# Weight tiles of half the size, and the squares of the residual behind all turning, in a two-layer trunk

## The chip, the cores and the metric

One core of one Trainium2 chip runs the whole program, eight cores being there. The metric is the device time of one execution in microseconds, of which the median of several runs is given. The profile's span is counted from the first to the last instruction and is a little shorter than the execution it was taken of. Engines are named as in the profile: PE multiplies matrices (PEld loads its weights), ACT is the scalar engine, DVE the vector engine, POOL and SP here issue DMA.

## The reference

The input is x of 256 tokens by 2048. Layer 0 mixes tokens by a gated linear recurrence (HGRN2, 16 heads), layer 1 by gated linear attention (GLA, 4 heads), each in chunks of 64 tokens. Behind each mixer comes an MLP of width 8192 with a squared ReLU. Around each of the four sub-layers stand two norms and a residual:

```
for i in range(DEPTH):
    hn = rmsnorm(h, norm_mix_pre[i])
    m = hgrn2_mixer(hn, ...) if i % N_MIXERS == 0 else gla_mixer(hn, ...)   # ends in o @ w_out
    h = h + rmsnorm(m, norm_mix_post[i])
    f = sqrelu_mlp(rmsnorm(h, norm_mlp_pre[i]), mlp_w_up[i], mlp_w_down[i])
    h = h + rmsnorm(f, norm_mlp_post[i])

def sqrelu_mlp(h, w_up, w_down):
    u = jax.nn.relu(h @ w_up)
    return (u * u) @ w_down
```

All is float32, and all matrix products are wide: 2048 by 8192 (HGRN2's inputs), 2048 by 2048, 2048 by 6160 (GLA's inputs), and for each layer 2048 by 8192 and 8192 by 2048.

## The kernel before

**Splits.** PE multiplies a rounded float32 format. To keep float32's precision each operand is split into two: `hi`, a rounded copy, made by ACT (`split_hi`, line 113), and `lo`, the rest raw - hi, made by DVE (`split_lo`, line 117). A product is three matmuls, x_hi by w_hi, x_hi by w_lo and x_lo by w_hi (lines 145 to 147 in `mm_half`, line 171 and 174 in `gemmT` for products that come out turned). So every weight passes DMA, ACT and DVE before PE takes it.

**Chunks and halves.** The host lays the weights out in chunks of 1 MB, 128 partitions by 2048 numbers. `load_chunk` (line 107) takes a tile from the pool `wraw` and loads a whole chunk by one DMA from SP's queue; the pool has three such tiles. Everything behind it works in halves of 128 x 1024: a hi and a lo tile of this size come from the pool `wsp` (five of each). A raw tile can be loaded anew when the lo of its second half is made. Six kinds of loads use `wraw`, 364 whole chunks in all; SP's queue issues 435 DMAs.

**The MLP.** The rows of 256 tokens meet `w_up` in groups of eight chunks (`up`, `gemmT`). The product with `w_dn` is done block by block in a Strassen-like form, with seven products in place of eight (`seven`, line 659): some operands are sums of two weight blocks, made by DVE (line 696, 714) or by accumulating DMAs that POOL issues (line 638 `add_to`, line 650 `load_b12`) into tiles called `bs`. `step` and `plan` weave the two; the products are called sa, sb and sc.

**The passage** (`transition`, line 436) leads from the last quarter of columns of one sub-layer to the first product of the next. It is run three times: from HGRN2's output projection to MLP 0, from MLP 0 to GLA, and from GLA's output projection to MLP 1. The order on PE, ACT, DVE and POOL is written out by hand there (`manual_schedule(engines=ALL)`; SP isn't among them). For each half `t` of the tokens (128 rows): the last products (`last`), the norm (`first_use`, `post.rstd`), the four residual additions on DVE (`post.residual(n, t)`, line 386), the turning of the new residual in four blocks (`T_in(t, q)`: four transposes on PE into one of two PSUM banks, line 207; `T_out(t, q)`: split out of the bank by four instructions on ACT, line 218, and four on DVE, line 220), and then the products `nxt(t, j)`, j = 0 to 7, of the turned blocks with eight weight halves. These eight halves are split ahead (`Next`, `ahead.split()`): they go to rooms that lie idle then (sbig, sqk, sf, stt, saccA, srun in the profile), some to `wsp`. For the scale of the next norm the squares of the residual are summed on ACT (`square`, line 309, four per token half); `rstd_sum` needs all eight. `split_early` splits the first three halves of the sub-layer's own weights.

**Who sets the order elsewhere.** In `start` (line 235) a hand-written order includes SP. Everywhere else a scheduler orders the instructions of each engine by a simulated timeline, in which loads count too; so other tiles can move other instructions. Each engine's queue runs in its order.

Of the kernel before, what the change touches and what calls it, by code (L numbers as in the profile page):

```python
# [11 lines left out]
F32 = mybir.dt.float32  # L12
# [6 lines left out]
P = 128  # L19
# [11 lines left out]
def trunk(  # L31
# [7 lines left out]

    const = ctx.enter_context(tc.tile_pool(name="const", bufs=1))  # L40
    big = ctx.enter_context(tc.tile_pool(name="big", bufs=4))
    wraw = ctx.enter_context(tc.tile_pool(name="wraw", bufs=3))
    wsp = ctx.enter_context(tc.tile_pool(name="wsp", bufs=5))
    tokp = ctx.enter_context(tc.tile_pool(name="tok", bufs=12))
    halfp = ctx.enter_context(tc.tile_pool(name="half", bufs=6))
# [28 lines left out]
    def nm(s):  # L74
        uid[0] += 1
        return f"{s}_{uid[0]}"
# [26 lines left out]
    def load_chunk(wap, idx):  # L103
        if idx in ahead and ahead[idx][0] is wap:
            return ahead.pop(idx)[1]
        raw = wraw.tile([P, 2, 1024], F32, tag="raw", name=nm("raw"))
        nc.sync.dma_start(raw, wap[idx].rearrange("p (k n) -> p k n", k=2))
        return raw

    def split_hi(raw, into=None):  # L110
# [16 lines left out]
    def split_early(wap, idx, count):  # L127

        raw = load_chunk(wap, idx)
        early[wap.tensor.name, idx] = raw, [split(raw[:, hf, :]) for hf in range(count)]  # L130

    def split_chunk(wap, idx):

        raw, halves = early.pop((wap.tensor.name, idx), (None, []))
        if raw is None:
            raw = load_chunk(wap, idx)
        return halves + [split(raw[:, hf, :]) for hf in range(len(halves), 2)]

    def mm_half(ps, half, hf, xs, t, nk, kks=(0, 1), cs=slice(0, NB)):

# [94 lines left out]
    def start(which, w, base):  # L235

        X = Xhl(KT)
        xs = big.tile([P, KT, T], F32, tag="big", name="xs")  # L240
        ps = [psmm.tile([P, NB], F32, tag="mm", name=nm("mm")) for _ in range(NT)]
        first = []
        part = small.tile([P, NT, 4], F32, tag="tp", name=nm("tp"))
        new_residue()

        def input_quarters(t, qs):
            for q in qs:
                c = slice(q * NB, (q + 1) * NB)
                nc.sync.dma_start(hs(t, c), x[t * P:(t + 1) * P, c])
            for q in qs:  # L250
                square(part, t, q)

        def next_chunk(c):
            raw = wraw.tile([P, 2, 1024], F32, tag="raw", name=nm("raw"))
            for j in range(2):
                nc.sync.dma_start(raw[:, j, :], w[c].rearrange("p (k n) -> p k n", k=2)[:, j, :])
            ahead[c] = w, raw
            first.append(gemmT(w, c, X, *((psmm, "mm") if c < 2 else (pssc, "sc"))))

        with tc.manual_schedule(engines=ALL | {mybir.EngineType.SP}):  # L260
            for hf in range(KT // 2):
                if hf % 2 == 0:
                    raw = wraw.tile([P, 2, 1024], F32, tag="raw", name=nm("raw"))
                    src = w[base + hf // 2].rearrange("p (k n) -> p k n", k=2)
                for n in range(2 if hf == 0 else 1):

                    m = 2 if hf else 1
                    ks = slice(2 * hf + n, 2 * hf + n + m)
                    cs = slice(n * NB, (n + m) * NB)
                    lead = hf == 0 and n == 0  # L270
                    nc.sync.dma_start(xs[:, ks, :], xT[:, ks, :])
                    (nc.scalar if lead else nc.sync).dma_start(raw[:, hf % 2, cs], src[:, hf % 2, cs])
                    if lead:
                        nc.sync.dma_start(prew, npre)
                        A.activation(warm, epsb, AF.Sqrt)
                        for _ in range(4):
                            idle = pstr.tile([P, T], F32, tag="tr", name=nm("idle"))
                            PE.matmul(idle, bc(epsb, [P, P]), bc(epsb, [P, T]), start=True, stop=True)
                    for k in range(2 * hf + n, 2 * hf + n + m):
                        hi, lo = X.both(k)[:, 0, :], X.both(k)[:, 1, :]  # L280
                        g = prew[:, which, k:k + 1]
                        A.activation(hi, xs[:, k, :], AF.Copy, scale=g)
                        V.scalar_tensor_tensor(lo, xs[:, k, :], g, hi.bitcast(F32),
                                               ALU.mult, ALU.subtract)
                    if n == 0:
                        half = (wsp.tile([P, 1024], F32R, tag="hi", name=nm("hi")),
                                wsp.tile([P, 1024], F32R, tag="lo", name=nm("lo")))
                    A.activation(half[0][:, cs], raw[:, hf % 2, cs], AF.Copy)  # L288
                    V.tensor_tensor(half[1][:, cs], raw[:, hf % 2, cs],  # L289
                                    half[0][:, cs].bitcast(F32), ALU.subtract)  # L290
                    if hf == 0:
                        for t in range(NT):
                            mm_half(ps[t], half, hf, X, t, KT, (n,))
                if hf:
                    for t in range(NT):
                        mm_half(ps[t], half, hf, X, t, KT)
            next_chunk(0)
            next_chunk(1)
            input_quarters(0, (0, 1))
            next_chunk(2)  # L300
            input_quarters(0, (2, 3))
            nc.sync.dma_start(ident, ident_in)
            next_chunk(3)
            input_quarters(1, range(4))
            rs = rstd_sum(part)
        return X, rs, ps, first
# [81 lines left out]
    class Next:  # L388
# [27 lines left out]
                yield None  # L416

        def raw(self, j):
            return self.raws[j // 2][:, j % 2, :]

        def hi(self):
            j = len(self.parts)
            if j % 2 == 0:
                self.raws.append(load_chunk(self.w, self.base + j // 2))
            self.parts.append(split_hi(self.raw(j), next(self.room)))

        def lo(self):
# [8 lines left out]
    def transition(w, base, nk, xs, post, add, which, ahead):  # L436
# [20 lines left out]
        def nxt(t, j):  # L457
            mm_half(psn[t], ahead.parts[j], j, X, t, KT)
# [21 lines left out]
        with tc.manual_schedule(engines=ALL):  # L480
# [28 lines left out]
            nxt(0, 3)  # L509
            post.residual(1, 1)  # L510
            post.residual(2, 1)
            part = small.tile([P, NT, 4], F32, tag="tp", name=nm("tp"))
            for q in range(4):
                square(part, 0, q)
            nxt(0, 4)
            ahead.split()
            T_in(1, 0)
            T_out(1, 0)
            nxt(0, 5)
            T_in(1, 1)  # L520
            nxt(0, 6)
            T_out(1, 1)
            post.residual(3, 1)
            T_in(1, 2)
            nxt(0, 7)
            T_out(1, 2)
            T_in(1, 3)
            T_out(1, 3)
            for chunk in ahead.then:
                split_early(*chunk)  # L530
            for q in range(4):
# [7 lines left out]
    def mlp(layer, w_up, w_dn, X, rs, ps0, then=None, at_end=None):  # L539
# [119 lines left out]
        def seven(g, p, following):  # L659
# [9 lines left out]
                return lambda k: (sa[g][k][:, 0, c, :], sa[g][k][:, 1, c, :])  # L669

            def raw_of(h, n):
                raw = load_chunk(w_dn, n * 16 + 2 * g + h)
                return [raw[:, j, :] for j in range(2)]

            def product(b, x, raw, n, t, sign=1):
                banks, key = (through, p) if b == "c" else (bank, b)
# [587 lines left out]
```

## Time and profile before

| what | value |
|---|---|
| time, median of 3 runs | 2246.48 us (2246.0 to 2246.5) |
| the profiled execution | 2245.75 us, of which span 2244.0 us |
| granted clock of PE | 0.999 |
| DMA | 516.67 MB, mean 230 GB/s |
| queue q1 (SP's and ACT's loads) | 405.43 MB |
| queue q0 (POOL's) | 109.06 MB |

The page gives each engine's busy time. A busy PE alone says little here, since matmuls overlap: the waits of PE and of its weight loads, and the distance between the starts of matmuls, tell where it stood still. A wait is put down to the line and engine that ended it; a line that is a helper's, like 113 or 117, stands for all splits. In the timeline equal instructions that follow each other on an engine are one row, and what stands in brackets is the idle time ahead of it and what ended it.

### The profile page before, as it was taken

To read this page: it belongs to the slowest core of one execution; us is meant where nothing else is said; L and a number is where in the kernel's file an instruction comes from. 1 tells how busy PE (TensorE), PEld (TensorE's weight loads), DVE (VectorE), ACT (ScalarE), POOL (GpSimd) and SP (SyncE) were. 2 spreads that over 40 slices of the span, in tenths; PEclk is the share of its full clock that TensorE was granted. 3 is DMA by queue.
4 is the path that set the end of the run, shared out by engine and by line. 5 is a ranking of instruction groups with operands and counts; after the bars stand their busy time and mean duration, and the time that the engine had idled before them with its cause. 6 is when DMAs were issued, how large, how long until landed. Compare 5 with 4: busy or idle time off the path is not lost.

```text
span 2244.0 us, 30106 instructions
## 1 busy us (share of the span) xinstructions
PE 2229.9 (99%) x11380; PEld 1898.8 (85%) x11380; DVE 1823.2 (81%) x2503; ACT 1404.5 (63%) x1926; POOL 119.4 (5%) x162
## 2 busy tenths in 40 slices
PE   9999999999999999999999999999999999999998
PEld 7888888888888888888887888888888888888887
DVE  6887877667899899898886778666789989989886
ACT  7554555456666666676657456555766666667664
POOL 0000000000010110110000000000001010011000
PEclk9999999999999999999999999999999999999999
DMA  8545445457889889888863544465788988898885
GB/s 327 177 166 172 169 152 186 169 207 239 263 268 264 265 266 272 268 255 280 268 263 133 201 156 160 170 203 201 232 263 274 262 265 267 271 271 256 273 266 189
DMA packets 85233, 516.67 MB, mean 230 GB/s; under 512 B 10144, under 2 KB 10656, under 8 KB 32352
## 3 DMA queue, kind: packets, MB, share of 16 engines
q1 hardware_dynamic: 62192, 405.43, 49.7%
q0 software_dynamic: 22752, 109.06, 22.2%
q8 instruction: 89, 1.46, 0.3%
q14 instruction: 56, 0.46, 0.1%
q10 hardware_dynamic: 144, 0.26, 0.0%
HBM read 508.43 MB, written 6.29 MB: 229 GB/s over the span
## 4 chain that ended last, share of the span: by engine, by line
PE 92%; DVE 3%; DMA 3%; ACT 1%; issue 1%; SPq 0%; DVEq 0%; ACTq 0%
PE mmT L171 26%; PE mmT L174 13%; PE sa L687 12%; PE mm L146 9%; PE mm L147 9%; PE mm L145 9%; PE sb L687 6%; PE sc L687 3%; DMA raw<-w_up 2%; PE sc L858 2%; DVE lo L117 2%; ACT hi L113 1%; PE tr L207 1%; DMA raw<-w_dn 0%; PE sd L894 0%
## 5 line engine op out<-in xcount | busy, mean ns | idle before, releaser
L113 ACT ACTIVATE hi<-raw 128x1024 fp32r<-128x1024 f32 x718 | 751.4, 1058 | 534.5 <-PE mm L147 173.2
L117 DVE TENSOR_TENSOR lo<-raw,hi 128x1024 fp32r<-128x1024 f32 x718 | 865.1, 1220 | 259.9 <-ACT hi L113 192.2
L171 PE MATMUL mmT<-xhl,hi 128*128 128x512 f32 x2688 | 652.5, 391 | 0.8 <-ACT hi L113 0.7
L171 PEld LDWEIGHTS mmT<-xhl,hi 128*128 128x128 f32 x2688 | 499.4, 188 | 103.7 <-ACT hi L113 3.0
L174 PEld LDWEIGHTS mmT<-xhl,lo 128*128 128x128 f32 x2688 | 352.0, 191 | 16.1
L174 PE MATMUL mmT<-xhl,lo 128*128 128x256 f32 x2688 | 359.2, 283 | 0.0
L146 PE MATMUL mm<-lo,xhl 128*128 128x512 f32 (+1 forms) x896 | 349.5, 390 | 0.7 <-DVE lo L117 0.4
L145 PE MATMUL mm<-hi,xhl 128*128 128x512 f32 (+1 forms) x896 | 349.0, 391 | 1.2 <-ACT hi L288 0.6
L147 PE MATMUL mm<-hi,xhl 128*128 128x512 f32 (+1 forms) x896 | 347.7, 389 | 0.0
L113 ACT ACTIVATE hi<-bs 128x1024 fp32r<-128x1024 f32 x224 | 234.9, 1057 | 92.4 <-PE mmT L171 46.7
L117 DVE TENSOR_TENSOR lo<-bs,hi 128x1024 fp32r<-128x1024 f32 x224 | 270.4, 1219 | 13.7 <-PE mmT L174 8.8
L145 PEld LDWEIGHTS mm<-hi,xhl 128*128 128x128 f32 x896 | 168.9, 188 | 35.9 <-ACT hi L288 1.3
L146 PEld LDWEIGHTS mm<-lo,xhl 128*128 128x128 f32 x896 | 169.0, 189 | 35.4 <-DVE lo L289 1.4
L147 PEld LDWEIGHTS mm<-hi,xhl 128*128 128x128 f32 x896 | 168.7, 188 | 34.4 <-issue 0.3
L687 PE MATMUL sb<-hi,as 128*128 128x512 f32 x448 | 149.2, 390 | 0.0
L687 PE MATMUL sa<-hi,as 128*128 128x512 f32 x448 | 148.0, 391 | 0.0
L687 PE MATMUL sa<-hi,xhl 128*128 128x512 f32 x448 | 147.4, 390 | 0.0
L638 POOL DMA_DIRECT2D bs<-w_dn x100 | 87.3, 874 | 1012.0 <-DVE lo L117 561.6
L687 PEld LDWEIGHTS sa<-hi,xhl 128*128 128x128 f32 x448 | 84.2, 188 | 17.0
L687 PEld LDWEIGHTS sa<-hi,as 128*128 128x128 f32 x448 | 84.3, 188 | 16.3
L687 PEld LDWEIGHTS sb<-hi,as 128*128 128x128 f32 x448 | 84.3, 188 | 15.9
L687 PE MATMUL sb<-lo,as 128*128 128x512 f32 x224 | 87.9, 392 | 1.2 <-DVE lo L117 1.2
(236 smaller groups left out, 2180.1 us busy)
## 6 DMA issues: line engine op xcount, KB each, us to landing
raw<-w_up SPq DMA_DIRECT2D x128, 1024.0 KB, 5.7
raw<-w_dn SPq DMA_DIRECT2D x100, 1024.0 KB, 6.7
raw<-w_hin SPq DMA_DIRECT2D x56, 1024.0 KB, 4.9
bs<-w_dn POOLq DMA_DIRECT2D x112, 512.0 KB, 7.2
raw<-w_gin SPq DMA_DIRECT2D x48, 1024.0 KB, 4.9
bs<-w_dn POOLq DMA_DIRECT2D x44, 1024.0 KB, 8.4
raw<-w_hout SPq DMA_DIRECT2D x16, 1024.0 KB, 4.9
raw<-w_gout SPq DMA_DIRECT2D x16, 1024.0 KB, 4.9
```

The source lines that it names most:

```text
L113: A.activation(hi, raw, AF.Copy)
L117: V.tensor_tensor(half[1], raw, half[0].bitcast(F32), ALU.subtract)
L145: PE.matmul(ps, xh, hi[:, kk, cs], start=(k == 0), stop=False)
L146: PE.matmul(ps, xh, lo[:, kk, cs], start=False, stop=False)
L147: PE.matmul(ps, xl, hi[:, kk, cs], start=False, stop=(k == nk - 1))
L171: PE.matmul(ps, hi, X.both(k), start=(k == 0), stop=False)
L174: PE.matmul(ps[:, 0, :], lo, X.both(k)[:, 0, :], start=False, stop=(k == KT - 1))
L207: PE.transpose(ps[:, j, :], src(j), ident)
L638: nc.gpsimd.dma_start(raw, b, accum_op=ALU.add)
L687: PE.matmul(ps, l, r[:, kk, :], start=first and j + kk + i == 0, stop=j + kk + i == 4, skip_group_check=not first)
L858: PE.matmul(ps[:, hd, :], l(hd * kt + k), r(hd * kt + k), start=(k == 0), stop=(k == kt - 1))
```

## The change

It has two parts. The pool `wraw` gets six tiles of half a chunk in place of three of a whole one, and each half is loaded by a DMA of its own, of 512 KB; `load_chunk` returns a list of two tiles. `Next.hi` now loads only the half that it splits. In the passage, for the second token half, the four squares of the first token half go from ahead of that half's turning to behind it, the split `ahead.split()` goes from ahead of `T_in(1, 0)` to behind `T_out(1, 0)`, and the writing order of `nxt` and `T_out` becomes regular.

```diff
-    wraw = ctx.enter_context(tc.tile_pool(name="wraw", bufs=3))
+    wraw = ctx.enter_context(tc.tile_pool(name="wraw", bufs=6))
...
-        raw = wraw.tile([P, 2, 1024], F32, tag="raw", name=nm("raw"))
-        nc.sync.dma_start(raw, wap[idx].rearrange("p (k n) -> p k n", k=2))
+        return [load_half(wap[idx].rearrange("p (k n) -> p k n", k=2)[:, j, :]) for j in range(2)]
+
+    def load_half(src):
+        raw = wraw.tile([P, 1024], F32, tag="raw", name=nm("raw"))
+        nc.sync.dma_start(raw, src)
         return raw
...
-        return halves + [split(raw[:, hf, :]) for hf in range(len(halves), 2)]
+        return halves + [split(raw[hf]) for hf in range(len(halves), 2)]
...
         def hi(self):
             j = len(self.parts)
-            if j % 2 == 0:
-                self.raws.append(load_chunk(self.w, self.base + j // 2))
+            chunk = self.w[self.base + j // 2].rearrange("p (k n) -> p k n", k=2)
+            self.raws.append(load_half(chunk[:, j % 2, :]))
             self.parts.append(split_hi(self.raw(j), next(self.room)))
...
             post.residual(2, 1)
+            nxt(0, 4)
+            T_in(1, 0)
+            T_out(1, 0)
+            ahead.split()
+            nxt(0, 5)
+            T_in(1, 1)
+            T_out(1, 1)
+            post.residual(3, 1)
+            nxt(0, 6)
+            T_in(1, 2)
+            T_out(1, 2)
+            nxt(0, 7)
+            T_in(1, 3)
+            T_out(1, 3)
             part = small.tile([P, NT, 4], F32, tag="tp", name=nm("tp"))
             for q in range(4):
                 square(part, 0, q)
-            nxt(0, 4)
-            ahead.split()
-            T_in(1, 0)
-            T_out(1, 0)
-            nxt(0, 5)
-            T_in(1, 1)
-            nxt(0, 6)
-            T_out(1, 1)
-            post.residual(3, 1)
-            T_in(1, 2)
-            nxt(0, 7)
-            T_out(1, 2)
-            T_in(1, 3)
-            T_out(1, 3)
             for chunk in ahead.then:
                 split_early(*chunk)
```

`start`, `next_chunk` and `raw_of` are written to match: the first loads were cut into halves by DMA before, but into a tile of a whole chunk.

Three places in the built programs. The lines of the changed kernel are three higher (110 is its load, 116 and 120 are hi and lo) or one lower (308, 385) than those of before. The first is ACT's queue in the first passage, from the output projection to MLP 0. Before:

```order
357 L309 ACTIVATE tok_4437,tp_4436<-h_119 128x512
358 L309 ACTIVATE tok_4439,tp_4436<-h_119 128x512
359 L309 ACTIVATE tok_4441,tp_4436<-h_119 128x512
360 L309 ACTIVATE tok_4443,tp_4436<-h_119 128x512
361 L113 ACTIVATE hi_4451<-raw_4327 128x1024
362 L218 ACTIVATE xhl_4267<-tr_4455,prew 128x128 x4
363 L218 ACTIVATE xhl_4267<-tr_4474,prew 128x128 x4
364 L218 ACTIVATE xhl_4268<-tr_4494,prew 128x128 x4
365 L218 ACTIVATE xhl_4268<-tr_4513,prew 128x128 x4
366 L113 ACTIVATE hi_4528<-raw_4526 128x1024
```

And the same place of the change:

```order
358 L221 ACTIVATE xhl_4423<-tr_4600,prew 128x128 x4
359 L116 ACTIVATE hi_4615<-raw_4613 128x1024
360 L221 ACTIVATE xhl_4423<-tr_4625,prew 128x128 x4
361 L221 ACTIVATE xhl_4424<-tr_4645,prew 128x128 x4
362 L221 ACTIVATE xhl_4424<-tr_4664,prew 128x128 x4
363 L308 ACTIVATE tok_4678,tp_4677<-h_119 128x512
364 L308 ACTIVATE tok_4680,tp_4677<-h_119 128x512
365 L308 ACTIVATE tok_4682,tp_4677<-h_119 128x512
366 L308 ACTIVATE tok_4684,tp_4677<-h_119 128x512
367 L116 ACTIVATE hi_4690<-raw_4686 128x1024
```

The four squares (tok<-h) went from ahead of the four turned blocks (xhl<-tr) to behind them, and the split hi from ahead of block 0 to behind it. The same place on DVE, from the two residuals of the second token half on. Before:

```order
561 L386 SCALAR_TENSOR_TENSOR h_119<-tok_4175,col_4398,h_119 128x512
562 L117 TENSOR_TENSOR lo_4452<-raw_4327,hi_4451 128x1024
563 L220 SCALAR_TENSOR_TENSOR xhl_4267<-tr_4455,prew,xhl_4267 128x128 x4
564 L220 SCALAR_TENSOR_TENSOR xhl_4267<-tr_4474,prew,xhl_4267 128x128 x4
565 L386 SCALAR_TENSOR_TENSOR h_119<-tok_4383,col_4398,h_119 128x512
```

With the change:

```order
562 L385 SCALAR_TENSOR_TENSOR h_119<-tok_4323,col_4556,h_119 128x512
563 L223 SCALAR_TENSOR_TENSOR xhl_4423<-tr_4600,prew,xhl_4423 128x128 x4
564 L120 TENSOR_TENSOR lo_4616<-raw_4613,hi_4615 128x1024
565 L223 SCALAR_TENSOR_TENSOR xhl_4423<-tr_4625,prew,xhl_4423 128x128 x4
566 L385 SCALAR_TENSOR_TENSOR h_119<-tok_4541,col_4556,h_119 128x512
```

The split lo went behind block 0; the residual of the last quarter (row 565, now 566) still has the same work ahead of it. The third place is SP's queue within MLP 0, where loads of `w_up` and `w_dn` take turns. Before, one row is a chunk:

```order
156 L107 DMA raw_6895<-w_dn 128x2048
157 L107 DMA raw_6925<-w_up 128x2048
158 L107 DMA raw_7018<-w_up 128x2048
159 L107 DMA raw_7067<-w_dn 128x2048
160 L107 DMA raw_7098<-w_up 128x2048
```

With the change, two rows are one:

```order
278 L110 DMA raw_7139<-w_dn 128x1024
279 L110 DMA raw_7141<-w_dn 128x1024
280 L110 DMA raw_7171<-w_up 128x1024
281 L110 DMA raw_7173<-w_up 128x1024
282 L110 DMA raw_7266<-w_up 128x1024
283 L110 DMA raw_7268<-w_up 128x1024
284 L110 DMA raw_7317<-w_dn 128x1024
285 L110 DMA raw_7319<-w_dn 128x1024
286 L110 DMA raw_7350<-w_up 128x1024
287 L110 DMA raw_7352<-w_up 128x1024
```

The sequence of chunks is the same, and each half has its own row and so its own tile to wait for. The scheduler also changed the places of some splits and small PE groups in the MLPs and ahead of the passages; the amount of work on PE, ACT, DVE and POOL is the same.

More of the change, by code (lines that the diff above doesn't have):

```diff
@@ L129, in split_early @@
         raw = load_chunk(wap, idx)
-        early[wap.tensor.name, idx] = raw, [split(raw[:, hf, :]) for hf in range(count)]
+        early[wap.tensor.name, idx] = raw, [split(raw[hf]) for hf in range(count)]
     def split_chunk(wap, idx):
@@ L253, in next_chunk @@
         def next_chunk(c):
[L254 to L257, printed above, removed]
+            ahead[c] = w, load_chunk(w, c)
             first.append(gemmT(w, c, X, *((psmm, "mm") if c < 2 else (pssc, "sc"))))
@@ L261, in start @@
             for hf in range(KT // 2):
-                if hf % 2 == 0:
-                    raw = wraw.tile([P, 2, 1024], F32, tag="raw", name=nm("raw"))
-                    src = w[base + hf // 2].rearrange("p (k n) -> p k n", k=2)
+                raw = wraw.tile([P, 1024], F32, tag="raw", name=nm("raw"))
+                src = w[base + hf // 2].rearrange("p (k n) -> p k n", k=2)
                 for n in range(2 if hf == 0 else 1):
@@ L271, in start @@
                     nc.sync.dma_start(xs[:, ks, :], xT[:, ks, :])
-                    (nc.scalar if lead else nc.sync).dma_start(raw[:, hf % 2, cs], src[:, hf % 2, cs])
+                    (nc.scalar if lead else nc.sync).dma_start(raw[:, cs], src[:, hf % 2, cs])
                     if lead:
@@ L287, in start @@
                                 wsp.tile([P, 1024], F32R, tag="lo", name=nm("lo")))
-                    A.activation(half[0][:, cs], raw[:, hf % 2, cs], AF.Copy)
-                    V.tensor_tensor(half[1][:, cs], raw[:, hf % 2, cs],
+                    A.activation(half[0][:, cs], raw[:, cs], AF.Copy)
+                    V.tensor_tensor(half[1][:, cs], raw[:, cs],
                                     half[0][:, cs].bitcast(F32), ALU.subtract)
@@ L418, in raw @@
         def raw(self, j):
-            return self.raws[j // 2][:, j % 2, :]
+            return self.raws[j]
         def hi(self):
             j = len(self.parts)
-            if j % 2 == 0:
-                self.raws.append(load_chunk(self.w, self.base + j // 2))
+            chunk = self.w[self.base + j // 2].rearrange("p (k n) -> p k n", k=2)
+            self.raws.append(load_half(chunk[:, j % 2, :]))
             self.parts.append(split_hi(self.raw(j), next(self.room)))
@@ L671, in raw_of @@
             def raw_of(h, n):
-                raw = load_chunk(w_dn, n * 16 + 2 * g + h)
-                return [raw[:, j, :] for j in range(2)]
+                return load_chunk(w_dn, n * 16 + 2 * g + h)
             def product(b, x, raw, n, t, sign=1):
```

## The prediction

> **What bounds the kernel now.** The page comes first, then the windows of 50 us, then who waited for whom, and last the timeline at the waits.
>
> ```profile
> span 2244.0 us, 30106 instructions
> PE 2229.9 (99%) x11380; PEld 1898.8 (85%) x11380; DVE 1823.2 (81%) x2503; ACT 1404.5 (63%) x1926; POOL 119.4 (5%) x162
> ```
> ```profile
> 0.00:50.00 50.00, 48.14 (x214) 39.21 (x215) 32.03 (x56) 40.05 (x64) 0.20 (x4) 1.00 0.90 334
> 750.00:800.00 50.00, 49.81 (x258) 42.44 (x257) 44.09 (x54) 33.11 (x41) 6.41 (x8) 1.00 0.87 261
> 1500.00:1550.00 50.00, 50.00 (x222) 41.42 (x221) 33.26 (x35) 29.12 (x37) 0.00 (x0) 1.00 0.80 279
> 2200.00:2250.00 50.00, 36.29 (x183) 30.85 (x181) 28.30 (x42) 16.70 (x30) 0.00 (x0) 0.93 0.37 138
> ```
>
> A window's columns are its bounds, its length, the busy time (and instructions) of PE, PEld, DVE, ACT and POOL, the granted clock, the busy share of the 16 DMA engines and GB/s. PE is idle for 2244.0 - 2229.9 = 14.1 us. The first window holds 50 - 48.14 = 1.9 us of it, the last, which has 44 us of the run, 44.0 - 36.3 = 7.7 us: start and tail, which the change leaves alone. Between them lie 4.5 us. So no edit to loads or to other engines can win much; the clock is full. Busy PE hides a little more, since the ends of matmuls are modelled, so the pitch counts:
>
> ```profile
> 30.48 3.63 PE mmT L171 x16
> ```
>
> In this row of the chain of waits 16 matmuls of 512 columns take 3.63 us, 0.227 us each, though each shows some 0.39 us in the timeline. Where the next one starts later than 0.227 us after the last, PE stalled, idle or not. Who waited, first on PE, then on its weight loads, then on ACT (columns: total us, times, longest):
>
> ```profile
> PE tr L207 <- DVE xhl L220: 1.5, 4, 1.0
> PE sb L687 <- DVE lo L117: 1.2, 2, 0.6
> PE mmT L171 <- ACT hi L113: 0.7, 2, 0.5
> PE mm L146 <- DVE lo L117: 0.4, 1, 0.4
> ```
> ```profile
> PEld mmT L171 <- ACT hi L113: 3.0, 7, 0.9
> PEld sb L687 <- DVE lo L117: 2.5, 4, 1.0
> PEld mm L146 <- DVE lo L117: 0.9, 1, 0.9
> ```
> ```profile
> ACT hi L113 <- DMA raw<-w_up: 73.5, 13, 7.2
> ```
>
> PE waits for a split (hi on ACT, lo on DVE), the split for a load of `w_up`. One such place in the timeline, and its load in the chain:
>
> ```profile
> 757.39 1.22 DVE L117 TENSOR_TENSOR lo<-raw,hi 128x1024 fp32r<-128x1024 f32 x1
> ...
> 759.46 1.22 DVE L117 TENSOR_TENSOR lo<-raw,hi 128x1024 fp32r<-128x1024 f32 x1
> ...
> 760.71 3.80 SPq L107 DMA_DIRECT2D raw<-w_up  x2
> ...
> 762.93 3.49 DVE L117 TENSOR_TENSOR lo<-raw,hi 128x1024 fp32r<-128x1024 f32 x3
> ...
> 771.14 2.01 ACT L113 ACTIVATE hi<-raw 128x1024 fp32r<-128x1024 f32 x2 [6.94 <-DMA raw<-w_up]
> ...
> 771.68 0.39 PE L687 MATMUL sc<-hi,xhl 128*128 128x512 f32 x1
> ...
> 772.26 3.92 PE L171 MATMUL mmT<-xhl,hi 128*128 128x512 f32 x16 [0.19 <-ACT hi L113]
> ```
> ```profile
> 760.71 10.33 DMA raw<-w_up
> ```
>
> The load is issued at 760.71, right behind the lo that ends at 759.46 + 1.22 = 760.68: that was the second half of the chunk whose buffer it takes. It needs 10.33 us, ACT sits for 6.94 us, and PE, which had splits in hand, stalls by 772.26 - 771.68 - 0.227 = 0.35 us, between its idle 0.19 and the longer wait of its weight load.
>
> **The change, part by part.** *Halves.* The same bytes come in tiles of half a chunk, six in place of three. The first half's buffer is then free at 757.39 + 1.22 = 758.61, not at 760.68: its load is issued 2.07 us sooner, carries half the bytes, and ACT can start on it alone. The second half is issued when the chunk was. The longest of these PE waits is 1.0 us, so 2.07 us covers each. The three kinds of PE wait above add up to 1.2 + 0.7 + 0.4 = 2.3 us by PE's idle time, and to 3.0 + 2.5 + 0.9 = 6.4 us by its weight loads, which wait beside a running matmul. The pitch at 772.26 lies between the two, so I take the middle, **4.3 us saved**, and keep 0 and 6.4 as the ends. The waits of sb belong to it: there DVE is catching up after such a hold of ACT.
>
> Each chunk has one more load to issue and to wait for.
>
> ```profile
> 29.88 3.49 DVE L117 TENSOR_TENSOR lo<-raw,hi 128x1024 fp32r<-128x1024 f32 x3
> ```
> ```profile
> 774.63 0.33 SPq L107 DMA_DIRECT2D raw<-w_up  x1
> ```
> ```profile
> raw<-w_up SPq DMA_DIRECT2D x128, 1024.0 KB, 5.7
> raw<-w_hin SPq DMA_DIRECT2D x15, 512.0 KB, 7.6
> ```
>
> At 29.88 the chunks were already loaded half by half (line 256), and three lo take 3.49 us, as at 762.93 where they came whole: a wait for each half costs DVE nothing once the half is there. Behind a waiting hi stand only later splits and folds on ACT, whose half would have been waited for in any case. SP gets one more issue for each of 364 whole-chunk loads, 0.33 us each, 120 us over the whole span, on a queue with 435 issues (144 us) that otherwise waits for buffers: 0 us. If SP had no room, a load would be 0.33 us later, well inside the 2.07.
>
> Of the DMA itself: the opening window loads halves and moves 334 GB/s at a busy share of 0.90, 371 per full share; the window at 1500 loads whole chunks at 279 / 0.80 = 349. Halves cost the engines nothing that these rows show, and the busiest stage has 0.87. I take 0; the bad end is the fourth case below. [...]
>
> *The passage.* The squares issue no DMA; the split now issues its own half's load (before, the chunk had come whole with the split ahead of it), on SP, whose order isn't written by hand there and which has its buffer earlier than the split its place. In each of the three passages, four squares leave ACT's queue ahead of the second half's turning, and the split (hi and lo) slides from ahead of the first turned block of that half to behind it. The squares' own cost there is the stretch from 1177.90 to 1180.35, 2.45 us of ACT. Passage from MLP to GLA:
>
> ```profile
> 1177.90 0.67 ACT L309 ACTIVATE tok<-h 128x512 f32<-128x512 f32 x1
> ...
> 1178.99 0.60 PE L207 MATMUL tr<-ident,h 128*128 128x128 f32 x4
> ...
> 1180.35 1.08 ACT L113 ACTIVATE hi<-raw 128x1024 fp32r<-128x1024 f32 x1
> ...
> 1181.30 2.20 ACT L218 ACTIVATE xhl<-tr,prew 128x128 fp32r<-128x128 f32 x8
> ...
> 1182.61 2.15 DVE L220 SCALAR_TENSOR_TENSOR xhl<-tr,prew,xhl 128x128 fp32r<-128x128 f32 x8
> ...
> 1183.79 0.66 PE L207 MATMUL tr<-ident,h 128*128 128x128 f32 x4 [1.00 <-DVE xhl L220]
> ...
> 1184.68 0.74 DVE L386 SCALAR_TENSOR_TENSOR h<-tok,col,h 128x512 f32<-128x512 f32 x1
> ...
> 1185.67 0.60 PE L207 MATMUL tr<-ident,h 128*128 128x128 f32 x4
> ```
>
> Block 0 is turned by 1178.99 + 0.60 = 1179.59, but ACT takes it at 1181.30, behind squares and split; DVE is through with it after half of its 2.15 us, near 1183.7, and block 2, which needs that bank, waits 1.00 us. After the change ACT takes block 0 at 1179.6 and is done at 1180.8 (1.14 us a block, the row at 504.75 below), DVE 1.08 us later, 1181.9, ahead of the time at which PE wants the bank (1183.79 - 1.00 = 1182.8): that wait goes. What is late next: DVE then does lo (1.22), block 1 (1.08) and the last residual (0.74) in a row, 1181.9 + 3.0 = 1184.9, some 1185.0 with the hand-over, and block 3 can't be turned before. It was turned at 1185.67, so this passage wins **0.6 us**, not 1.0.
>
> In the two passages behind an output projection ACT had time for the squares:
>
> ```profile
> 504.75 1.14 ACT L218 ACTIVATE xhl<-tr,prew 128x128 fp32r<-128x128 f32 x4
> ...
> 508.79 0.74 DVE L386 SCALAR_TENSOR_TENSOR h<-tok,col,h 128x512 f32<-128x512 f32 x1
> ...
> 509.59 0.65 PE L207 MATMUL tr<-ident,h 128*128 128x128 f32 x4
> ...
> 511.30 2.97 ACT L113 ACTIVATE hi<-raw 128x1024 fp32r<-128x1024 f32 x3
> ```
> ```profile
> 520.99 1.29 PE L171 MATMUL mmT<-xhl,hi 128*128 128x512 f32 x5
> ```
>
> ACT takes block 0 at 504.75, straight after it is turned; nothing is to be won. Now hi (1.08) comes behind it, 505.9 to 507.0; DVE has block 0 to 507.0, lo to 508.2, block 1 to 509.3, and the residual runs to 510.0, not 509.53. Block 3 was turned at 509.59, right behind it, and so comes **0.5 us** later, twice. The squares now follow the last turning, ahead of the early splits, which start at 511.30 + 0.5 + 2.45 = 514.3 and end at 517.2; PE first needs them at 520.99, so 3.8 us of cover are left and they cost nothing. Without that cover it would be 2.45 us a passage.
>
> **Sum.** -4.3 (loads) - 0.6 + 2 x 0.5 (passages) = -3.9 us. The profiled execution took 2245.75 us, so 2241.9 for it; its median of three lies 0.7 us higher, 2246.48, hence **2242.6 us**.
>
> **The rivals.** *More goes* (0.17): with halves every one of those waits vanishes at the weight loads too, 6.4 us, and -6.4 + 0.4 gives 2240.5. For it: 2.07 us is more than each wait. Against: the wait of a weight load is partly beside a running matmul.
> *The loads are no earlier* (0.20): the 10.33 us come from engines that are 0.87 busy with the accumulating loads too, not from a late issue; then only the passages count, +0.4: 2246.9. Against: a load that is half as long and issued sooner must end sooner unless something else is pushed ahead of it.
> *Half loads land later* (0.08, the slower side): the 512 KB rows landed in 7.6 us, `w_up`'s chunks in 5.7, so 1.9 us longer. The second half is issued when the chunk was; if it is late by that much where ACT has no lead, PE's stall grows by as much. Seven places (the count at mmT) x 1.9 = 13.3 us: 2260. It decides as soon as a half lands later than its chunk did. Against: those 512 KB loads landed in the opening crowd at 0.90. [...]
>
> **Chances.** My forecast gets 0.55, from 2241.0 to 2244.5. A measurement of this kernel tells 0.2%, 4.5 us, from no change, so faster means under 2242.0. Of the forecast 0.12 lies there, with the 0.17 of the first rival 0.29. Within: 0.43 + 0.20 = 0.63. Slower: 0.08. The range 2240.0 to 2247.5 leaves out the slow case, half of the first rival and a little beyond the second.
>
> **What would show it.** In the profile after: ACT's waits for `w_up` well under 73.5 us and none near 7; PE's waits for hi and lo from loads gone (if they stand, the second rival; if longer, the third); in the MLP to GLA passage no 1.00 us before a turning by DVE's block, but a short one for the residual at block 3 in all three. Wrong would also be a stall at a place where there was none: other instructions were reordered with the loads, and I have counted that as nothing.

## The result, and the profile after

| | before | after |
|---|---|---|
| median of 6 runs, in turn on one chip | 2246.89 us (2246.0 to 2248.82) | 2258.32 us (2257.22 to 2260.48) |
| ratio, 95% interval | | 1.0051 (1.0040 to 1.0061) |
| span of the profiled execution | 2244.0 us | 2256.2 us |

The change makes the kernel 11.4 us slower; 2242.6 was predicted. The page's first lines of the changed kernel show as little as they did before:

```profile
span 2256.2 us, 31260 instructions
PE 2233.2 (99%) x11380; PEld 1901.1 (84%) x11380; DVE 1823.7 (81%) x2503; ACT 1408.7 (62%) x1926; POOL 119.8 (5%) x162
```

PE is now idle for 2256.2 - 2233.2 = 23.0 us instead of 14.1, and 3.3 us longer busy with the same 11380 matmuls. Who waited on PE, and for whom (total us, times, longest):

```profile
PE mmT L174 <- DVE tok L590: 7.3, 2, 4.3
PE mm L148 <- ACT hi L116: 1.8, 1, 1.8
...
PE sb L685 <- DVE lo L120: 1.4, 2, 0.9
...
PE tr L210 <- DVE h L385: 0.6, 3, 0.2
```

Two waits of the first row are new: `unfold` (line 590, tok<-mmT) frees a PSUM bank and comes late. The waits that were forecast to go are gone, but for sb's (1.4 us in 2, 1.2 before). DVE's own waits name a transfer that kept nobody waiting there before; two of the four are shown below, in MLP 0, the other two (4.15 and 2.99 us) stand at the same place in MLP 1:

```profile
DVE bs L694 <- DMA raw<-w_dn: 17.1, 4, 6.0
```

The n-th matmul writes the same tile in both kernels, but for 142 of the 11380, which the scheduler moved, so the difference of its starts tells where the time went (worked out from the two traces; times are those of before):

| stretch | us lost |
|---|---|
| opening, to 20 | +1.8 |
| 20 to 533 | -0.5 |
| **start of MLP 0, 533 to 554** | **+6.6** |
| 554 to 942 | -1.3 |
| 942 to 1130 (its end holds the 1.8 us wait of the second row) | +2.1 |
| 1130 to 1197, with the passage into GLA | -1.5 |
| 1197 to 1584 | +0.4 |
| **start of MLP 1, 1584 to 1616** | **+4.7** |
| 1616 to the last matmul | +0.1 |

The opening runs in an order written by hand that all kernels below with half tiles share; their profiles show -0.2 to 1.84 us there, so it isn't counted as an effect of the change. What is left, in the main, are the starts of the two MLPs. The timeline of DVE at the start of MLP 0 after the change (start, length, operation; in brackets the idle time ahead and what ended it):

```profile
536.11 1.23 DVE L694 TENSOR_TENSOR bs<-raw,bs 128x1024 f32<-128x1024 f32 x1 [5.95 <-DMA raw<-w_dn]
537.25 1.22 DVE L120 TENSOR_TENSOR lo<-raw,hi 128x1024 fp32r<-128x1024 f32 x1
...
545.32 1.23 DVE L694 TENSOR_TENSOR bs<-raw,bs 128x1024 f32<-128x1024 f32 x1 [3.98 <-DMA raw<-w_dn]
546.46 2.36 DVE L120 TENSOR_TENSOR lo<-raw,hi 128x1024 fp32r<-128x1024 f32 x2
...
550.47 0.42 DVE L590 TENSOR_TENSOR tok<-mmT,half 128x256 f32<-128x256 f32 x1
```

And of the kernel before at the same place:

```profile
539.11 2.35 DVE L696 TENSOR_TENSOR bs<-raw,bs 128x1024 f32<-128x1024 f32 x2
...
543.11 0.42 DVE L591 TENSOR_TENSOR tok<-mmT,half 128x256 f32<-128x256 f32 x1
```

Before, both additions run without a wait and the first unfold starts at 543.11; after, each addition waits for its half of `w_dn`, and the first unfold starts at 550.47, 7.4 us later (1.4 of them were lost before this place). SP's queue tells why there are two waits and not one:

```profile
530.19 8.64 SPq L110 DMA_DIRECT2D raw<-w_dn  x2
```

A row of two issues ends with the second: half 0 was asked for at 530.19, half 1 only at 530.19 + 8.64 - 0.33 = 538.50, right behind the lo of 537.25, which ends at 538.47. That lo frees half 1's tile (in the program half 1 goes to the place in SBUF that this lo reads), and it stands behind the addition that waits for half 0. PE, which needs a bank for its next product, meanwhile:

```profile
550.94 5.30 PE L174 MATMUL mmT<-xhl,hi 128*128 128x512 f32 x15 [4.32 <-DVE tok L590]
```
```profile
1622.37 5.52 PE L174 MATMUL mmT<-xhl,hi 128*128 128x512 f32 x16 [2.97 <-DVE tok L590]
```

PE idles 4.32 and 2.97 us, and then 16 matmuls take 5.52 us (the view of the first row ends ahead of its sixteenth). In the kernel before, the same row of the timeline shows 3.82:

```profile
1617.25 3.82 PE L171 MATMUL mmT<-xhl,hi 128*128 128x512 f32 x16
```

The clock had fallen. Windows of the changed kernel (columns as in the prediction):

```profile
548.00:552.00 4.00, 1.06 (x3) 0.88 (x4) 4.00 (x9) 1.64 (x4) 0.00 (x0) 0.89 0.87 141
552.00:556.00 4.00, 4.00 (x14) 3.18 (x13) 3.34 (x14) 4.00 (x12) 0.00 (x0) 0.69 0.66 252
1616.00:1620.00 4.00, 3.40 (x25) 3.04 (x23) 3.25 (x3) 2.27 (x4) 0.88 (x1) 1.00 0.68 228
1623.00:1627.00 4.00, 4.00 (x12) 3.19 (x11) 3.27 (x13) 4.00 (x11) 0.00 (x0) 0.59 0.79 286
```

In MLP 1, 2.97 us of idle time and 5.52 - 3.82 = 1.7 us of slow clock are the 4.7 us of the table. In both MLPs the next product starts 5.37 us after the first of these matmuls (556.31 and 1627.74), where it was 3.66 us before, so MLP 0 loses 1.7 us by the clock too, and idle time and clock together make 4.32 + 2.97 + 2 x 1.7 = 10.7 of the 11.4 us. The queue of DVE at the start of MLP 0, in numbered rows of the two programs; before:

```
587 L117 TENSOR_TENSOR lo_4879<-raw_4872,hi_4878 128x1024
588 L696 TENSOR_TENSOR bs_4973<-raw_4971,bs_4691 128x1024
589 L696 TENSOR_TENSOR bs_4973<-raw_4971,bs_4692 128x1024
590 L215 TENSOR_TENSOR xhl_4609<-tr_4640,xhl_4609 128x4x128
591 L117 TENSOR_TENSOR lo_4925<-raw_4922,hi_4924 128x1024
592 L591 TENSOR_TENSOR tok_4650<-mmT_4651,half_4684 128x256
```

With the change:

```
585 L694 TENSOR_TENSOR bs_5147<-raw_5143,bs_4855 128x1024
586 L120 TENSOR_TENSOR lo_4989<-raw_4982,hi_4988 128x1024
587 L218 TENSOR_TENSOR xhl_4773<-tr_4792,xhl_4773 128x4x128
588 L120 TENSOR_TENSOR lo_5045<-raw_5040,hi_5044 128x1024
589 L120 TENSOR_TENSOR lo_5049<-raw_5042,hi_5048 128x1024
590 L694 TENSOR_TENSOR bs_5147<-raw_5145,bs_4856 128x1024
591 L120 TENSOR_TENSOR lo_5097<-raw_5092,hi_5096 128x1024
592 L120 TENSOR_TENSOR lo_5101<-raw_5094,hi_5100 128x1024
593 L218 TENSOR_TENSOR xhl_4773<-tr_4804,xhl_4773 128x4x128
594 L120 TENSOR_TENSOR lo_5154<-bs_5147,hi_5153 128x1024
595 L590 TENSOR_TENSOR tok_4814<-mmT_4815,half_4848 128x256
```

The scheduler now has a separate ready time for each half. It put the first addition ahead of a lo (row 586) that used to be ahead of both, and two splits, one more of the next chunk (row 592) and that of the sum (row 594, from bs), ahead of the unfolds; before, three of the four unfolds stood ahead of both. In the timeline above DVE takes these rows in the order of its queue, from row 585 at 536.11 us to row 595 at 550.47, so everything below a row that waited came later too. ACT's queue has the same thing at the end of MLP 0 (the wait of 1.8 us):

```profile
1128.49 1.06 ACT L116 ACTIVATE sbig<-raw 128x1024 fp32r<-128x1024 f32 x1 [4.94 <-DMA raw<-w_gin]
1129.46 1.04 ACT L116 ACTIVATE hi<-bs 128x1024 fp32r<-128x1024 f32 x1
1130.40 1.04 ACT L116 ACTIVATE hi<-raw 128x1024 fp32r<-128x1024 f32 x1
```

The split of the next stage's first half (sbig) waits for `w_gin`; behind it stand the hi's that PE needs at once.

### The profile page after: what moved, and what is told of

Read it like the earlier page. It is cut to its first block, busy times and chain, and to the rows that moved or that the text cites. A ratio compares the mean times of both kernels' runs of the same rounds, so it can differ in the third digit from the quotient of the medians.

```text
span 2256.2 us, 31260 instructions
## 1 busy us (share of the span) xinstructions
PE 2233.2 (99%) x11380; PEld 1901.1 (84%) x11380; DVE 1823.7 (81%) x2503; ACT 1408.7 (62%) x1926; POOL 119.8 (5%) x162
## 4 chain that ended last, share of the span: by engine, by line
PE 93%; DVE 3%; DMA 2%; ACT 1%; issue 1%; SPq 0%; DVEq 0%; ACTq 0%
PE mmT L174 26%; PE mmT L177 13%; PE sa L685 12%; PE mm L148 9%; PE mm L149 9%; PE mm L150 9%; PE sb L685 6%; PE sc L685 3%; PE sc L856 2%; DMA raw<-w_up 2%; DVE lo L120 1%; ACT hi L116 1%; PE tr L210 1%; DVE xhl L223 1%; PE sd L892 0%
```

## The experiments

Theory T: the scheduler places the first users of a half too early into queues that run in order, and what stands behind them is late. Rivals: P, the passage's later squares delay the MLP; D, half loads themselves cost the DMA queue. Three more came up on the way: N, the loss comes wherever the queues are ordered anew; C, the first addition's wait holds up the load that the second one waits for; Q, what counts is how late the unfolds come. Each run was measured in turn with the kernel before on one chip, and the ratio is to it; the chips differ between runs. The diffs are shortened: conditions that the text names, and the unwrapping of an instruction for `issue_after`, are left out.

| run | median us | ratio (95%) |
|---|---|---|
| half tiles, old passage | 2251.02 | 1.0019 (1.0011 to 1.0028) |
| new passage, whole chunks | 2245.97 | 0.9999 (0.9990 to 1.0008) |
| all pairs joined | 2257.58 | 1.0052 (1.0039 to 1.0065) |
| all pairs joined, old passage | 2258.76 | 1.0049 (1.0036 to 1.0061) |
| first pair joined | 2246.51 | 1.0000 (0.9991 to 1.0009) |
| first pair joined, old passage | 2245.66 | 0.9999 (0.9990 to 1.0007) |
| both pins | 2243.66 | 0.9988 (0.9979 to 0.9997) |
| both pins, old passage | 2243.13 | 0.9987 (0.9978 to 0.9996) |
| addition behind the split | 2253.71 | 1.0027 (1.0016 to 1.0038) |
| half loads, whole tiles | 2244.59 | 0.9988 (0.9979 to 0.9997) |
| splits behind the unfolds | 2248.35 | 1.0003 (0.9994 to 1.0011) |
| both moves | 2246.60 | 0.9996 (0.9987 to 1.0005) |

**Each part alone.** Half tiles with the passage's order of before, that is the change without its edit to `transition`:

```diff
+            part = small.tile([P, NT, 4], F32, tag="tp", name=nm("tp"))
+            for q in range(4):
+                square(part, 0, q)
             nxt(0, 4)
+            ahead.split()
             T_in(1, 0)
             T_out(1, 0)
-            ahead.split()
...
```

> Half tiles as in the changed kernel, the passage's squares where they stood before. Theory T (in each MLP the two additions that open the first pair of blocks stand apart in VectorE's queue, each waits for its half of w_dn, and the unfolds behind them free PSUM banks late): the waits of VectorE at about 536 and 545 us stay, and the time is 2256 to 2259, as of the whole change. Rival P (the later squares delay the start of the MLP): the waits go and the time is 2243 to 2248. Rival D (half loads cost the DMA queue itself): 2256 to 2259 too, and this run alone cannot tell D from T.

```profile
PE mmT L174 <- DVE tok L590: 4.0, 2, 3.0
```

2251.0 us: half tiles alone lose, but less than half of what the change loses, so no number was met, neither that of T and D nor P's. The two waits for the bank are there, shorter (3.0 and 1.05 us against 4.32 and 2.97). The passage alone, that is the change without this:

```diff
-    wraw = ctx.enter_context(tc.tile_pool(name="wraw", bufs=6))
+    wraw = ctx.enter_context(tc.tile_pool(name="wraw", bufs=3))
...
-        return [load_half(wap[idx].rearrange("p (k n) -> p k n", k=2)[:, j, :]) for j in range(2)]
+        raw = wraw.tile([P, 2, 1024], F32, tag="raw", name=nm("raw"))
+        nc.sync.dma_start(raw, wap[idx].rearrange("p (k n) -> p k n", k=2))
...
```

> Whole chunks as before, the passage in its new order. T and D: within 1 us of the kernel before (2246 to 2248), with the bank wait of 1.0 to 1.2 us in the passage into the GLA gone and short waits for the last residual in its place. P: about 2256 to 2258.

```profile
PE tr L207 <- DVE h L386: 0.5, 3, 0.2
```

2246.0 us, no difference, as T and D said: the passage by itself costs nothing, so P as a cause by itself falls. Its own two effects came as forecast: the bank wait went, and three short waits for the last residual took its place. In its profile the matmuls run 1.6 us ahead of the kernel before at 1616 us and 0.7 behind it at the end, with one new wait of 1.2 us for a hi at 1839 us; so the new passage, too, let the scheduler change other places, and the zero is a sum.

**Joining the additions.** In `seven`, line 693 on:

```diff
-            for j in range(2):
-                V.tensor_tensor(run[j], b11[j], q[j], ALU.add)
+            second = V.tensor_tensor(run[1], b11[1], q[1], ALU.add)
+            with tc.issue_after(second):
+                V.tensor_tensor(run[0], b11[0], q[0], ALU.add)
```

> The changed kernel with one difference: the addition of the second half is placed first and that of the first half right behind it, so that unfolds stand ahead of both in VectorE's queue. T: the idle stretches of TensorE before the first matmuls at the start of both MLPs (4.3 and 3.0 us, and the slow matmuls behind them) go, the time falls by 8 to 11 us, to 2247 to 2250. D: unchanged, 2257 to 2259, with the idle time in other places. P: unchanged.

> Half tiles, the two additions joined as in the run before, and the squares of the passage where they stood before the change. T: 8 to 11 us under the changed kernel, 2246 to 2250; what lies between this run and the one before it is the passage's share, expected under 1 us either way. D: 2257 to 2259. P: 2243 to 2248, and clearly faster than the run before it.

```profile
PE mmT L174 <- ACT hi L116: 10.2, 10, 2.1
```

Both missed: 2257.6 and 2258.8. The wait for unfold is gone from PE's list and the start of MLP 0 loses nothing (the same matmuls lag by 0.8 us at 537 and at 573 us), but joining all 28 pairs let the scheduler order the whole MLPs anew, and ten new waits for a hi came up. These two runs changed too much to decide anything; D's number was met by accident, as the next two show, where only the first pair of each MLP is joined:

```diff
+            if g == 0 and p == 0:
+                second = V.tensor_tensor(run[1], b11[1], q[1], ALU.add)
+                with tc.issue_after(second):
+                    V.tensor_tensor(run[0], b11[0], q[0], ALU.add)
+            else:
...
```

> The changed kernel with the two additions joined in the first pair of each MLP alone; all other pairs keep their order (in the earlier run with joined additions the start of MLP 0 lost 0.5 us instead of 6.5, but joining all pairs let ten new waits for w_up appear later, up to 2.1 us each). T: the stretch up to the 3600th matmul loses under 1 us against the kernel before, no new waits follow, and the time is 2247 to 2251, 7 to 11 us under the changed kernel. Rival N (the loss is not in these two places but comes wherever the halves let the queues be ordered anew): the start of the MLPs is repaired but others take its place, 2254 to 2260.

> Half tiles with the passage of before and the two additions joined in the first pair of each MLP alone. T: 3 to 5 us under the run with half tiles alone (2251.0), 2245 to 2248. N: 2251 to 2258.

```profile
537.10 1.23 DVE L694 TENSOR_TENSOR bs<-raw,bs 128x1024 f32<-128x1024 f32 x1 [1.82 <-DMA raw<-w_dn]
538.24 1.22 DVE L696 TENSOR_TENSOR bs<-raw,bs 128x1024 f32<-128x1024 f32 x1
...
542.25 0.41 DVE L590 TENSOR_TENSOR tok<-mmT,half 128x256 f32<-128x256 f32 x1
```

2246.5 us with the new passage, 11.8 under the changed kernel, and 2245.7 with the old one: one wait instead of two, and the first unfold (first kernel, above) at 542.25 instead of 550.47. That is T; of the times one lies 0.5 us under its range and the other in it. D and N fall. All the half loads are still there. Now the other place, the end of `mlp`, where `last_hi[0]` is the hi written last before it:

```diff
             if ahead is not None:
-                ahead.split(1)
+                with tc.issue_after(last_hi[0]):
+                    ahead.split(1)
```

> As the changed kernel with the first pair's additions joined, and in addition the first split of w_gin in MLP 0's last part is queued on ScalarE behind the splits of w_dn that stand before it in the code. T: the wait of TensorE of 1.8 us at about 1129 goes, 1 to 2.5 us under the run without this pin, 2243 to 2249. N: unchanged or slower.

> Both pins with the passage of before. T: 1 to 2.5 us under the run with one pin and the old passage, 2243 to 2247, and what is between this run and the one before it is the passage's own share with no misplaced waits. N: unchanged or slower.

Each lies 2.5 to 2.9 us under its run without the pin (1 to 2.5 were expected), and PE's wait at 1129 is gone from its list (new passage):

```profile
PE sb L687 <- DVE lo L122: 1.0, 2, 0.5
...
PE tr L212 <- DVE h L387: 0.6, 3, 0.2
```

These are the fastest of the runs, 0.12% and 0.13% under the kernel before, with intervals that exclude 1. The passages differ by 0.5 us, inside what the runs tell.

**Which of the moved rows.** Joining the pair also moved other rows (the splits of rows 592 and 594 went behind three unfolds, as in the kernel before). To take that apart, first only the addition:

```diff
-            for j in range(2):
-                V.tensor_tensor(run[j], b11[j], q[j], ALU.add)
+            with tc.issue_after(los[-5]):
+                V.tensor_tensor(run[0], b11[0], q[0], ALU.add)
+            V.tensor_tensor(run[1], b11[1], q[1], ALU.add)
```

`los` lists the lo's in the order of the code; `los[-5]` is the one of row 586. This holds for the first pair; the others stay.

> The changed kernel with two swaps of neighbouring rows in VectorE's queue at the start of each MLP and every row of TensorE and ScalarE as it was: the addition of the first half comes one row later, behind the split that frees the tile which the second half of w_dn is loaded into, and the addition of the second half one row earlier. The additions stay apart by two other rows. Theory C (a closed chain: the addition waits for half 0, behind it stands the split that frees half 1's tile, so half 1 is asked for only when half 0 has landed, and the next addition waits again): SyncE issues the second half of w_dn 3 to 5 us earlier, at about 534 instead of 538.5, the second wait of VectorE falls from 4.0 us to under 1, TensorE's idle time of 4.3 and 3.0 us goes, and the time is 2245 to 2250. Theory T in its plain form (additions that stand apart and early each wait, whatever stands between): first wait unchanged, second wait over 2 us, TensorE still idle for 2 us or more in each MLP, 2252 to 2258.

```profile
530.18 5.12 SPq L110 DMA_DIRECT2D raw<-w_dn  x2
```
```profile
536.85 1.22 DVE L698 TENSOR_TENSOR bs<-raw,bs 128x1024 f32<-128x1024 f32 x1 [1.90 <-DMA raw<-w_dn]
...
539.72 1.22 DVE L699 TENSOR_TENSOR bs<-raw,bs 128x1024 f32<-128x1024 f32 x1
...
545.38 1.22 DVE L122 TENSOR_TENSOR lo<-raw,hi 128x1024 fp32r<-128x1024 f32 x1 [2.17 <-ACT hi L116]
...
548.25 0.41 DVE L592 TENSOR_TENSOR tok<-mmT,half 128x256 f32<-128x256 f32 x1
```

The chain that C named is shown and broken: half 1 is issued at 530.18 + 5.12 - 0.33 = 534.97 instead of 538.50, and its addition doesn't wait. But the time, 2253.7, is not C's (it is the plain T's, whose second wait isn't there): the split of row 592 now waits 2.17 us, the unfolds stand behind it, and PE idles 2.48 us in each MLP. The view puts this wait down to a hi, but the hi that the row needs had ended at 542.11 + 1.07 = 543.18:

```profile
542.11 1.07 ACT L116 ACTIVATE hi<-raw 128x1024 fp32r<-128x1024 f32 x1 [0.49 <-PE mmT L176]
```
```profile
543.73 0.63 PE L179 MATMUL mmT<-xhl,lo 128*128 128x256 f32 x4
...
544.56 1.68 PE L179 MATMUL mmT<-xhl,lo 128*128 128x256 f32 x12
```

In the program the row waits for PE as well: it writes into the lo tile that the first eight of these 16 matmuls read, and the eighth ends at 545.28. That fits its start at 545.38. The split that was queued too early thus waited 2.17 us for PE's own work, and the unfolds that PE needed next waited behind it. The idle time and the slow clock that follows it in MLP 1 (1.7 us, last section) make 2 x 2.48 + 1.7 = 6.7 of the 7.2 us over the kernel before. So there are two causes in a row. The other one alone, with the additions as in the change and, for the chunk that `up(1)` takes first, its second split queued behind the third of the four unfolds (the scheduler then put rows 589, 591 and 594 behind all four as well), and both:

```diff
-        return halves + [split(raw[hf]) for hf in range(len(halves), 2)]
+        one, two = split(raw[0]), split_hi(raw[1])
+        with tc.issue_after(unfolds[-2]):
+            split_lo(raw[1], two)
+        return [one, two]
```

> The changed kernel; the two additions stay early and apart as in it, and three splits (the last half of the chunk before, both halves of the next chunk of w_up) stand behind the four unfolds instead of ahead of them, as one of the next chunk's did before. Theory Q (what counts is how late the first unfold ends against TensorE's need of its bank at about 546.6 us): the additions wait as in the changed kernel, the second until about 545, the first unfold ends at about 547 instead of 550.8, TensorE idles under 1 us in each MLP with its clock kept, and the time is 2247 to 2251. Rival (the additions' waits alone cost what was lost): 2254 to 2258.

```profile
535.10 1.23 DVE L706 TENSOR_TENSOR bs<-raw,bs 128x1024 f32<-128x1024 f32 x1 [5.14 <-DMA raw<-w_dn]
...
544.33 1.23 DVE L706 TENSOR_TENSOR bs<-raw,bs 128x1024 f32<-128x1024 f32 x1 [5.13 <-DMA raw<-w_dn]
...
546.07 0.42 DVE L600 TENSOR_TENSOR tok<-mmT,half 128x256 f32<-128x256 f32 x1
```

> Both moves: the first addition behind the split that frees half 1's tile, and the three splits behind the unfolds. Theory Q: the first unfold ends by about 543, no wait of TensorE for a bank at the start of either MLP, 2245 to 2249, as with the joined additions (2246.5). If order at these places is not the whole cause: above 2251.

Both times came as Q said. In the run with both moves the first unfold ends at 545.1, where 543 was expected, and a wait of 0.35 us for the bank stays in each MLP where none was expected. In the run with the splits alone the waits of the additions are as long as in the changed kernel, 10.3 us in all against 9.9, and yet 10 us come back, since the unfolds have less ahead of them. The edit let the scheduler move rows behind this place as well, but none ahead of it. In one table (first unfold of MLP 0, PE's idle time for its bank in MLP 0 and MLP 1):

| kernel | first unfold | PE idle | median |
|---|---|---|---|
| changed | 550.47 | 4.32, 2.97 | 2258.3 |
| addition behind the split | 548.25 | 2.48, 2.48 | 2253.7 |
| half tiles, old passage | 546.74 | 2.97, 1.05 | 2251.0 |
| splits behind the unfolds | 546.07 | 0.58, 0.35 | 2248.4 |
| both moves | 544.70 | 0.35, 0.35 | 2246.6 |
| first pair joined | 542.25 | none | 2246.5 |

The profiles reach this place up to 1.9 us apart, which shifts their first column but not their idle times. The less PE idles there in all, the shorter the run. The third line says what the passage adds to half tiles: against it the changed kernel idles 3.3 us longer and, unlike it, loses 1.7 us by the clock in each MLP, together 6.7 of the 7.3 us between the two runs. The scheduler's order differs there too: with the old passage the splits of rows 592 and 594 stand behind three unfolds, as in the kernel before, which takes some 2.4 us of DVE's work from ahead of them. The later squares and this order weren't taken apart at this place; but with the first pair joined, where both passages have these two splits behind the unfolds, the runs differ by less than 1 us (2246.5 and 2245.7).

**Where the gain of the halves comes from.** The kernel before with two loads per chunk, but into one whole tile:

```diff
-        nc.sync.dma_start(raw, wap[idx].rearrange("p (k n) -> p k n", k=2))
+        for j in range(2):
+            nc.sync.dma_start(raw[:, j, :], wap[idx].rearrange("p (k n) -> p k n", k=2)[:, j, :])
```

> The kernel before with each chunk of weights loaded by two transfers into the two halves of one whole tile (three tiles, passage as before). If the gain of the halves comes from a tile that is free sooner: no gain here, 2245.5 to 2248.5, and at least five of the seven waits for w_up in TensorE's queue between 600 and 2100 us remain; the closed chain can't occur, since both transfers wait for the same tile. If it comes from a first half that lands sooner in any tile: 2242 to 2244. If 364 more transfers on SyncE cost time by themselves: above 2249.

```profile
760.28 4.32 SPq L108 DMA_DIRECT2D raw<-w_up  x4
```
```profile
768.79 1.06 ACT L114 ACTIVATE hi<-raw 128x1024 fp32r<-128x1024 f32 x1 [5.01 <-DMA raw<-w_up]
770.05 1.06 ACT L114 ACTIVATE hi<-raw 128x1024 fp32r<-128x1024 f32 x1 [0.20 <-DMA raw<-w_up]
```

2244.6 us, 0.12% under the kernel before and just above the second case's range, and PE's waits that end at 772, 1138 and 2087 us before are gone. This is the place that the prediction worked through: the load is issued at 760.28, where the whole chunk was at 760.71, and ACT starts at 768.79, where it started at 771.14, 1.9 us sooner after the issue. So the gain doesn't need a tile that comes free sooner; a first half that lands sooner is enough. 364 more issues cost nothing that can be measured. The scheduler's order changed in this kernel as well, without a new wait of PE over 1 us; what part of the 0.12% this order has isn't shown.

## Why the prediction was wrong

The step that failed is its last sentence: "other instructions were reordered with the loads, and I have counted that as nothing". It was +11 us: the first-pair join, which keeps every load and the whole passage, brings 11.8 us back. The prediction had the rule in hand and looked at the wrong queue: "Behind a waiting hi stand only later splits and folds on ACT". True of ACT's hi for `w_up`; it didn't ask what stands behind a waiting addition on DVE, nor behind a waiting sbig on ACT. The rows were there in the two programs before any run; a term was owed for the additions, and for the splits moved ahead of the unfolds, at the start of both MLPs. It would have had to hold the slow clock too, 3.4 us that came behind the idle time.

- *Halves, -4.3 us (0 to 6.4).* Right in sign, smaller in size, and with one of its two reasons not needed. With both places pinned the whole change gives 2243.7, 2.5 us under the kernel before (0.7 to 4.7 by the interval); with the old passage 3.0. The waits named for it went, but for part of sb's. The earlier landing of the first half is enough for that, as the run with half loads into whole tiles shows; what the buffer that is free 2.07 us sooner adds isn't shown.
- *"a wait for each half costs DVE nothing once the half is there"*: right by its own condition, and the condition is what failed; the halves of `w_dn` weren't there, by 5.95 and 3.98 us.
- *SP's 364 more issues, 0; the DMA itself, 0.* Borne out: half loads into whole tiles are faster, not slower (2244.6 us against 2246.55). After the change:

```profile
raw<-w_up SPq DMA_DIRECT2D x256, 512.0 KB, 6.0
raw<-w_dn SPq DMA_DIRECT2D x200, 512.0 KB, 6.5
```

  Halves of `w_up` land in 6.0 us where chunks took 5.7, halves of `w_dn` in 6.5 where chunks took 6.7, and two halves are on their way at once: at 750.56, for one, two halves of `w_up` are asked for within 2.36 us.
- *Passage into GLA, -0.6; the other two, +0.5 each.* In the run with the passage alone, the lead of the same matmuls changes by -0.8 from 1179 to 1188 us, and by +0.35 at each of the others. The sum, -0.1 instead of +0.4, is within 0.5.
- *Later squares hidden by 3.8 us of cover.* Right for the passage alone. The cover was counted to PE's first need, not to the loads and unfolds that hang on the splits behind the squares; in the changed kernel the chain ahead of the unfolds ends later than with the old passage. How much of that is the squares and how much the order is open; where the order is repaired, the passage costs less than 1 us.
- *ACT's waits for `w_up` well under 73.5 us and none near 7*: wrong as a sign to look for. They are 77.3 us in 17, the longest 6.8, and PE's waits went all the same.
- *More goes, 2240.5; the loads are no earlier, 2246.9.* Neither: with both places pinned sb still waits twice, 1.0 us in all, and in the run with half loads into whole tiles ACT starts on a first half 1.9 us sooner after its issue.
- *The third rival, half loads that land later, 2260*: near the time, for another reason. At its place PE's weight loads waited less for a hi, 1.1 us in 3 after the change and 3.0 in 7 before; D, its like, fell with the first-pair join and the whole tiles.

## What to carry to other kernels

Where a scheduler orders in-order queues, a finer transfer is a new ready time, and its first user may be moved ahead of work that did not wait before: read in the changed program which rows newly stand behind a user of the transfer, above all those that free the tile of the next one or a PSUM bank, and price them. A load that waits for a tile whose release stands behind the wait for another load can bring a second wait, here 3.98 us behind one of 5.95. A change that loses by that may keep its gain with pinned rows, as here (2243.7 us with both pins), or by splitting the load and not the tile (2244.6 us).

## What the runs showed of the hardware

A PE that stands still for a few us can lose more than that: behind 2.97 us of idle time at 1622 us, 16 matmuls of 512 columns took 5.52 us instead of 3.82, at a granted clock of 0.59. It doesn't follow from the length alone. In the run with half tiles and the old passage PE idled 2.97 us too, just ahead of this window, and kept its clock:

```profile
548.00:552.00 4.00, 4.00 (x23) 3.41 (x22) 4.00 (x10) 4.00 (x10) 0.00 (x0) 1.00 0.97 266
```

In the run with the addition behind the split PE idled 2.48 us twice. In MLP 0, where the idle time reaches into this window, the clock stayed:

```profile
548.00:552.00 4.00, 3.28 (x14) 2.74 (x15) 3.33 (x13) 3.28 (x10) 0.00 (x0) 1.00 0.94 365
```

In MLP 1 of the same execution it fell:

```profile
1618.26 5.52 PE L176 MATMUL mmT<-xhl,hi 128*128 128x512 f32 x16 [2.48 <-DVE tok L592]
```
```profile
1619.00:1623.00 4.00, 4.00 (x12) 3.10 (x12) 3.16 (x12) 4.00 (x11) 0.00 (x0) 0.57 0.11 45
```

It fell behind the longest gap too, the 4.32 us in MLP 0 of the changed kernel (0.69 in the window from 552 us). Gaps of 2.97 and of 2.48 us were each followed once by a clock that fell (0.59 and 0.57) and once by one that stayed at 1.00. Why equal gaps fare differently, and how short a gap can still cost the clock, is not shown.
